# Decoder step on one core: the third and fourth delta-rule unit 14 and 10 slots later, convolution blocks alternating between them, two steps of every unit a slot further apart

## Chip, core and metric

One core of one Trainium2 chip. The metric is the device time of one launch in microseconds (us), the median of three runs. The core has a matrix engine (PE, with its weight loads as PEld), two vector engines (DVE, and POOL, which is GpSimd), a scalar engine for activation functions (ACT), and SP, which here only issues DMAs. Each engine runs its own instructions in order and waits on semaphores for the others.

## What is computed

One layer of a decoder step for 256 prompt tokens and 8 sample tokens, model width 2048. Four token mixers run in parallel on one input projection, their outputs are gated, summed and projected, then come cross-attention and a squared-ReLU MLP.

```python
proj = x @ p["w_in"] + p["b_in"]
...
o_a, S_a_new = gated_delta_rule(q_a, k_a, v_a, beta, g, S_a)        # A, 8 heads, chunks of 64
u_b, conv_b_new = causal_dwconv(a_b * jax.nn.sigmoid(g_b), conv_b, p["b_conv_w"])   # B, width 31
u_c, conv_c_new = causal_dwconv(cg_c * h_c, conv_c, p["c_conv_w"])  # C, width 3
h, C_new, n_new, m_new = mlstm_chunked(q, k, v, i_d.astype(f32), ...)               # D
y = jnp.sum(gates * proj_br, axis=2) @ p["w_out"]
```

In branch A each chunk needs `qk`, a lower triangular system `a_low`, its inverse, and then a recurrence over the four chunks of the prompt.

## The kernel before

All big products are cut into 704 **slots**. A slot is one 512 KB piece of weights (`raw`, 128 x 1024 floats) that SP loads, ACT rounds to `wh`, and DVE (for every fourth slot POOL) reduces to the rest `wl = raw - wh`; PE then does 24 matmuls with it (`xh*wh`, `xl*wh`, `xh*wl` for 8 blocks of 128). Splitting runs two slots ahead of the matmuls. `gin` is an input projection of 128 columns: two slots and a `post` that takes the result from PSUM.

Beside the slots stand Python generators. Once per slot the loop in `run` takes one step of the first generator of `chain`, and as many steps of `fill` as a planned DVE time (`dv_t` against `pe_t`, costs in `cost`) allows; a planned DVE time that is too far ahead skips the step of `chain` in that slot. `drain` takes all remaining steps of a generator at once. What the steps emit is then put in each engine's order by the tile scheduler, so a step's instructions can stand some slots behind the slot in which they were emitted.

- `a_gemm(u)` projects the six blocks (q, k, v of two heads) of unit `u` and `a_block` post-processes each: a width-4 convolution (`cu` on DVE), a sigmoid, a product on POOL. After the sixth, `a_unit(u)` is put on `chain`. There are four units, 0 to 3 (the third and fourth of the title are units 2 and 3); only one is in progress at a time. `a_begin(u)` drains unit `u - 2`, since two buffers `qkv` are shared by the four.
- `a_unit` first normalises q and k (`unit_rms`: a square and a split on ACT and POOL, the sums `ssl2q`, `ssl2k` on PE, logarithm and exponential on ACT, a DVE product), then computes `KQ` and decays, builds `m_u`, `m_a`, `m_t` on DVE, inverts in five levels (`xb`, then `ub` and `tb`), and runs the four chunks (`ks`, `db`, `ob`, `sb`), in between the state update of the samples (`s_upd`, which reads `dbc` from a DMA), and last a norm (`ssrm`). `unit_rms` keeps its result in a tile `rr` of which there is one.
- `b_block(j)` (two `gin`, four slots) puts `b_conv(j)` on `fill`: 30 DVE instructions `cB` of 128 x 256. `c_block(j)` has three `gin`, six slots, and little DVE work.
- `phase2(2, "C", True)` follows, from slot 128 on: gates by a sigmoid on ACT (`gate`) and a `merged` product on DVE, with no convolutions.

Slots before: unit 0 has slots 0 to 11, unit 1 12 to 23, blocks 0 and 1 of B and C 24 to 43, unit 2 44 to 55, blocks 2 to 4 56 to 85, unit 3 86 to 97, blocks 5 to 7 98 to 127.

Of the kernel before, what the change touches and what calls it, by code (L numbers as in the profile page):

```python
# [91 lines left out]
def decoder_step(ctx, tc, A, O):  # L92
# [15 lines left out]
    def bank(name):  # L108
        return pb.tile([P, 512], F32, tag="b", name=name)
# [6 lines left out]
    def cost(ap, rate=1.0):  # L116
        n = 1
        for x in ap.shape[1:]:
            n *= x
        dv_t[0] += 0.07 + n * rate / 960.0  # L120

    def act(out, in_, func, bias=0.0, scale=1.0, **kw):
        return AC.activation(out, in_, func, bias=bias, scale=scale, **kw)  # L123

    def tt(out, a, b, op, eng=None):
        if eng is None:
            cost(out)
        return (eng or DV).tensor_tensor(out=out, in0=a, in1=b, op=op)  # L128

    def ts(out, a, s1, op0, s2=None, op1=None):  # L130
        cost(out, 0.6)
        if op1 is None:
            DV.tensor_scalar(out, a, s1, None, op0=op0)
        else:
            DV.tensor_scalar(out, a, s1, s2, op0=op0, op1=op1)

    def stt(out, a, s, b, op0, op1):
        cost(out, 1.1)
        return DV.scalar_tensor_tensor(out=out, in0=a, scalar=s, in1=b, op0=op0, op1=op1)  # L139
# [9 lines left out]
    def mm(out, lhsT, rhs, start=True, stop=True):  # L149
        PE.matmul(out, lhsT, rhs, start=start, stop=stop)  # L150
# [3 lines left out]
    def split(hi, lo, src):  # L154
        act(hi, src, AF.Copy)
        tt(lo, src, hi.bitcast(F32), SUB)
# [9 lines left out]
    def sigmoid(g, src, bias=None):  # L166
        if bias is None:
            ts(g, src, -80.0, MAX)
        else:
            ts(g, src, bias, ADD, -80.0, MAX)  # L170
        act(g, g, AF.Exp, scale=-1.0)
        act(g, g, AF.Ln, bias=ones[:, 0:1])
        act(g, g, AF.Exp, scale=-1.0)
# [17 lines left out]
    def col(name, i=0, n=1):  # L191
        o, w = _pc[name]
        return pc[:, o + i:o + i + n]

    def con(name):
        o, w = _cc[name]
        return cst[:, o:o + w]
# [25 lines left out]
    def drain(g):  # L223
        for q in (chain, fill):
            while g in q:
                step(q)
# [12 lines left out]
    def later(n, f):  # L239
        todo.append((now[0] + n, f))  # L240

    def store(dst, src):
        later(DELAY, lambda: dma(dst, src))
# [127 lines left out]
    def gin(start, post):  # L371
        i = BI[start]
        gemm(A["win"][i - 1], xs, 2, lambda ps: post(ps, col("bin", i)))
# [63 lines left out]
    c1 = w1.tile([P, 2, 4, 8], F32, name="c1")  # L437
    c2 = w1.tile([P, 2, 4, 8], F32, name="c2")
    c3 = w1.tile([P, NCH, 2], F32, name="c3")
# [155 lines left out]
    def sconv(win, wc, W, dst, eng=None):  # L595
        t = tp.tile([P, NS, W], F32, tag="cw%d" % W, name="cw", bufs=1)
        tt(t[:], win, wc[:, None, :].to_broadcast([P, NS, W]), MUL, eng=GP)
        DV.reduce_sum(out=dst, in_=t[:], axis=AX.X)
        cost(t[:])
# [8 lines left out]
    def selc(h):  # L608
        return selw[:, h, :]
# [45 lines left out]
    def colb(ct, g, h, n, shape):  # L655
        return ct[:, :, g, h:h + n, None].to_broadcast(shape)

    def mat(name):
        return w1.tile([P, 2, 2, CH], F32, tag=name, name=name)

    def each():
        for hf in range(2):
            for hh in range(2):
                for c in range(2):
                    yield hf, hh, slice(CH * c, CH * c + CH), slice(hf * P + c * CH, hf * P + c * CH + CH)

    def v4(b):
        return b[:, :256].rearrange("p (f h l) -> p f h l", f=2, h=2)
# [19 lines left out]
    def a_unit(u):  # L688
# [7 lines left out]
        yield from unit_rms(k, 1.0, "l2k", res)  # L696
        tt(k, k, res[1][:], MUL)
        yield
        G = bank("G")[:].rearrange("p (h s f l) -> p h s f l", h=2, s=2, f=2)
        KQ = bank("KQ")[:].rearrange("p (f h s l) -> p f h s l", f=2, h=2, s=2)  # L700
        for hh in range(2):
            mm(G[:, hh], selc(h0 + hh), RA[:])
        Gs = [G[:, :, s].rearrange("p h f l -> p f h l") for s in range(2)]
        for hf, hh, o, t in each():
# [17 lines left out]
        for dst, src, m in ((U, U, "m1u"), (T, Am, "m1t")):  # L722
            tt(dst[:], src[:], con(m)[:, None, None, :].to_broadcast(sh), MUL)
            tt(dst[:], dst[:], con("eye")[:, None, None, :].to_broadcast(sh), ADD)
        yield
        sv = [P, 2, 2, P]
        v5 = lambda b: b[:].rearrange("p (f h l) -> p f h l", f=2, h=2)
# [164 lines left out]
    def newpair(name):  # L892
        return xp.tile([P, 2, NB, NT], F32R, tag="x16", name=name)
# [3 lines left out]
    def c_block(j):  # L897
        st = {}

        def post_h(ps, bc):  # L900
            if j == 0:
                drain(rowg[0])
                pr["C"] = newpair("pairC")
            st["h"] = tp.tile([P, NT], F32, tag="ht", name="ht", bufs=1)
            act(st["h"][:], ps, AF.Identity, bias=bc)

        def post_c(ps, bc):
            e = tp.tile([P, 30 + NT], F32, tag="ext", name="extC", bufs=1)
            GP.memset(e[:, 0:2], 0.0)
            stt(e[:, 2:2 + NT], ps, bc, st["h"][:], ADD, MUL)  # L910
            GP.tensor_copy(winC[:, j, :, 2], e[:, 2 + NP:2 + NT])
            GP.tensor_copy(scp[:, j, :], e[:, NP:NP + 2])
            wc = col("cC", 3 * j, 3)
            v = tp.tile([P, NT], F32, tag="cu", name="cuC", bufs=1)
            act(v[:, 0:NP], e[:, 0:NP], AF.Copy, scale=wc[:, 0:1])
            for i in range(1, 3):
                stt(v[:, 0:NP], e[:, i:i + NP], wc[:, i:i + 1], v[:, 0:NP], MUL, ADD)
            sconv(winC[:, j], wc, 3, v[:, NP:])
            st["v"] = v

        def post_b(ps, bc):
            v = st["v"]
            stt(v[:], ps, bc, v[:], ADD, MUL)
            split(pr["C"][:, 0, j, :], pr["C"][:, 1, j, :], v[:])
            if j == NB - 1:
                store(O["sc_p"], scp[:])
                store(O["sc_s"], winC[:])

        gin(O_H + P * j, post_h)
        gin(O_CG + P * j, post_c)  # L930
        gin(O_BG + P * j, post_b)
# [19 lines left out]
    def win_b(j):  # L951
        bst["w"] = tp.tile([P, NS, 31], F32, tag="winB", name="winB", bufs=2)
        dma(bst["w"][:], A["sB"][:, j])

    def b_block(j):
        st = {}

        def post_a(ps, bc):
            if j == 0:
                bst["cB"] = w1.tile([P, NB, NT], F32, tag="h8", name="cB", bufs=2)  # L960
                bst["ln"] = Norm(bst["cB"], NB, "B", w1, True)
            st["a"] = tp.tile([P, NT], F32, tag="ht", name="at", bufs=1)
            act(st["a"][:], ps, AF.Identity, bias=bc)

        def post_g(ps, bc):
            if j >= 2:
                drain(bgen[j - 2])
            g = tp.tile([P, NT], F32, tag="sg", name="gB")
            sigmoid(g[:], ps, bc)
            e = tp.tile([P, 30 + NT], F32, tag="extB", name="extB")  # L970
            win = bst["w"]
            if j < NB - 1:
                later(3, lambda: win_b(j + 1))
            GP.memset(e[:, 0:30], 0.0)
            tt(e[:, 30:], st["a"][:], g[:], MUL, eng=GP)
            GP.tensor_copy(win[:, :, 30], e[:, 30 + NP:])
            store(O["gl_p"][:, j], e[:, NP:NP + 30])
            store(O["gl_s"][:, j], win[:])
            dst = bst["cB"][:, j, NP:]
            sconv(win, col("cB", 31 * j, 31), 31, dst)  # L980
            ts(dst, dst, col("bcb", j), ADD)
            bgen[j] = b_conv(j, e)
            fill.append(bgen[j])

        gin(O_GLU + P * j, post_a)
        gin(O_GLU + BW + P * j, post_g)
# [84 lines left out]
    def d_unit(u):  # L1071
# [4 lines left out]
        KQ = v4(bank("KQd"))  # L1076
        G = bank("Gd")[:, :256].rearrange("p (h f l) -> p h f l", h=2, f=2)
        for hh in range(2):
            mm(G[:, hh], selc(h0 + hh), RD[:])
        for hf, hh, o, t in each():  # L1080
            mm(KQ[o, hf, hh], k[:, hh, t], q[:, hh, t])
        E, QK = mat("m_dl"), mat("m_dt")
        tt(E[:], G.rearrange("p h f l -> p f h l"), colb(c1, 3, h0, 2, sh), SUB)
        ts(E[:], E[:], 0.0, MAX)
# [180 lines left out]
        for i in range(4 if u == 0 else 0, 6):  # L1265
            gin(O_QKV + P * ((i // 2) * 8 + 2 * u + i % 2), a_block(u, i))

    def bc(js):
        for j in js:
            b_block(j)  # L1270
            c_block(j)

    a_gemm(0)
    a_gemm(1)
    bc((0, 1))
    a_gemm(2)
    bc((2, 3, 4))
    a_gemm(3)
    bc((5, 6, 7))
    phase2(2, "C", True)  # L1280
    bng = b_norm()
    mark(lambda: chain.append(bng))
# [570 lines left out]
```

## Time and profile before

| | us |
|---|---|
| median of three runs (2324.32 to 2328.25) | 2326.68 |
| the profiled execution, device time | 2324.7 |
| its span in the trace | 2322.9 |

What is read below comes from the profiled execution. The mean granted clock of PE is 0.990 of full speed in it. Slot numbers are counted from the weight matmuls in the trace, 24 to a slot: the blocks of unit 2 begin at 170 us, those of unit 3 at 336 us, phase 2 at 495 us, slot 176 at 665 us.

### The profile page before, as it was taken

The page shows a single profiled execution, that of the slowest core. Times are in us where ns is not written, and L with a number is a line of the kernel's source. Part 1 is how long each engine was busy: PE and PEld are TensorE (multiplying, and loading weights), DVE is VectorE, ACT ScalarE, POOL GpSimd, SP SyncE. Part 2 cuts the span into 40 slices and gives each one's busy share as a digit, 9 for nine tenths or more (in the row PEclk, how much of TensorE's full clock was granted, in tenths as well). Part 3 has the DMA queues.
Part 4 walks back from the last instruction along what each step waited for, and adds up shares of the span by engine and source line. Part 5 has one row for each costly group of instructions (what it writes and reads, how often), then busy time and mean ns, then how long its engine had stood idle before and what let it go on. Part 6 is the DMA issues. An engine that isn't in the chain of part 4 may idle for free.

```text
span 2322.9 us, 46442 instructions
## 1 busy us (share of the span) xinstructions
PE 2249.0 (97%) x19034; PEld 2205.4 (95%) x19034; DVE 1269.8 (55%) x2039; ACT 1167.0 (50%) x1789; POOL 977.8 (42%) x733
## 2 busy tenths in 40 slices
PE   9899999989999999999989999989999999999997
PEld 8899898989999999999989998889999999999997
DVE  7998998894464455433474566385323323323323
ACT  6756456554554455544434555456435435534543
POOL 4535335341222133433243365165445544544576
PEclk9999999999999999999999999999999999999998
DMA  7556455554656676765556666545565565566553
GB/s 233 166 151 201 137 174 167 169 165 143 193 173 185 195 221 215 211 182 182 182 183 182 200 200 201 187 132 181 181 182 176 179 182 181 174 183 181 176 180 127
DMA packets 125134, 418.81 MB, mean 180 GB/s; under 512 B 15608, under 2 KB 20984, under 8 KB 124920
## 3 DMA queue, kind: packets, MB, share of 16 engines
q1 hardware_dynamic: 124920, 415.84, 58.4%
q8 instruction: 149, 2.44, 0.4%
q14 instruction: 65, 0.53, 0.1%
HBM read 401.37 MB, written 14.41 MB: 179 GB/s over the span
## 4 chain that ended last, share of the span: by engine, by line
PE 81%; DVE 13%; issue 3%; DMA 1%; ACT 1%; POOL 1%; DVEq 0%; POOLq 0%; ACTq 0%; SPq 0%
PE g L150 73%; DVE cB L139 3%; DVE wl L128 3%; PE q L150 1%; DVE cu L139 1%; DVE y L128 1%; PE pv L150 1%; DVE y L139 1%; DMA dbc<-dd 1%; PE ub L150 0%; PE xb L150 0%; DVE s L139 0%; PE cb L150 0%; ACT wh L123 0%; PE nb L150 0%
## 5 line engine op out<-in xcount | busy, mean ns | idle before, releaser
L123 ACT ACTIVATE wh<-raw 128x1024 fp32r<-128x1024 f32 (+1 forms) x705 | 745.4, 1058 | 822.4 <-PE g L150 306.3
L128 POOL TENSOR_TENSOR wl<-raw,wh 128x1024 fp32r<-128x1024 f32 x240 | 588.0, 2450 | 724.7 <-PE g L150 483.2
L150 PE MATMUL g<-xh,wl 128*128 128x264 f32 x2496 | 714.0, 286 | 8.1 <-DVE wl L128 6.0
L150 PE MATMUL g<-xl,wh 128*128 128x264 f32 x2496 | 717.2, 287 | 0.0
L150 PE MATMUL g<-xh,wh 128*128 128x264 f32 x2496 | 716.1, 287 | 0.9 <-ACT wh L123 0.9
L128 DVE TENSOR_TENSOR wl<-raw,wh 128x1024 fp32r<-128x1024 f32 (+1 forms) x465 | 589.8, 1269 | 231.2 <-PE g L150 169.6
L150 PEld LDWEIGHTS g<-xh,wl 128*128 128x128 f32 x2496 | 473.0, 190 | 10.2 <-DVE wl L128 6.6
L150 PEld LDWEIGHTS g<-xh,wh 128*128 128x128 f32 x2496 | 473.5, 190 | 5.3 <-issue 2.5
L150 PEld LDWEIGHTS g<-xl,wh 128*128 128x128 f32 x2496 | 472.2, 189 | 2.3 <-issue 1.3
L150 PE MATMUL g<-hgh,wl 128*128 128x264 f32 x1024 | 290.4, 284 | 0.0
L150 PE MATMUL g<-hgl,wh 128*128 128x264 f32 x1024 | 290.4, 284 | 0.0
L150 PE MATMUL g<-hgh,wh 128*128 128x264 f32 x1024 | 289.9, 284 | 0.0
L150 PE MATMUL g<-zh,wh 128*128 128x266 f32 x960 | 275.1, 287 | 0.8 <-DVE zw L128 0.8
L150 PE MATMUL g<-zl,wh 128*128 128x266 f32 x960 | 274.6, 286 | 0.0
L150 PE MATMUL g<-zh,wl 128*128 128x266 f32 x960 | 274.4, 286 | 0.0
L150 PEld LDWEIGHTS g<-hgl,wh 128*128 128x128 f32 x1024 | 193.0, 188 | 0.0
L150 PEld LDWEIGHTS g<-hgh,wh 128*128 128x128 f32 x1024 | 192.5, 188 | 0.0
L150 PEld LDWEIGHTS g<-hgh,wl 128*128 128x128 f32 x1024 | 192.4, 188 | 0.0
L128 DVE TENSOR_TENSOR y<-y,g 128x264 f32<-128x264 f32 x80 | 34.3, 429 | 278.7 <-PE g L150 278.7
L150 PEld LDWEIGHTS g<-zh,wh 128*128 128x128 f32 x960 | 181.4, 189 | 1.0 <-ACT wh L123 1.0
L150 PEld LDWEIGHTS g<-zl,wh 128*128 128x128 f32 x960 | 181.7, 189 | 0.0
L150 PEld LDWEIGHTS g<-zh,wl 128*128 128x128 f32 x960 | 180.8, 188 | 0.0
(481 smaller groups left out, 3449.3 us busy)
## 6 DMA issues: line engine op xcount, KB each, us to landing
raw<-in_win_dram SPq DMA_DIRECT2D x312, 512.0 KB, 4.0
raw<-in_f_dram SPq DMA_DIRECT2D x248, 512.0 KB, 4.2
raw<-in_wbr_dram SPq DMA_DIRECT2D x64, 512.0 KB, 4.0
raw<-in_wout_dram SPq DMA_DIRECT2D x32, 512.0 KB, 4.3
s<-in_sS_dram SPq DMA_DIRECT2D x8, 512.0 KB, 5.0
dbc<-dd SPq DMA_DIRECT2D x16, 256.0 KB, 3.7
out_S_s_dram<-s SPq DMA_DIRECT2D x8, 512.0 KB, 5.2
c<-in_sCm_dram SPq DMA_DIRECT2D x8, 512.0 KB, 5.7
```

Source lines behind the costliest of these rows:

```text
L123: return AC.activation(out, in_, func, bias=bias, scale=scale, **kw)
L128: return (eng or DV).tensor_tensor(out=out, in0=a, in1=b, op=op)
L139: return DV.scalar_tensor_tensor(out=out, in0=a, scalar=s, in1=b, op0=op0, op1=op1)
L150: PE.matmul(out, lhsT, rhs, start=start, stop=stop)
```

## The change

Two steps get one slot more distance: an empty `yield` between the product that ends k's norm and `KQ`, and one between the building of `m_u`, `m_t` and the first level. A unit so has 38 steps where it had 36. And the order of the projections is another: blocks of B and C are still alternated, but seven of them now stand before unit 2, five between unit 2 and unit 3, four behind.

```diff
         tt(k, k, res[1][:], MUL)
         yield
+        yield
         G = bank("G")[:].rearrange("p (h s f l) -> p h s f l", h=2, s=2, f=2)
...
             tt(dst[:], dst[:], con("eye")[:, None, None, :].to_broadcast(sh), ADD)
+        yield
         yield
...
-    def bc(js):
-        for j in js:
-            b_block(j)
-            c_block(j)
+    def bc(order):
+        for f in order.split():
+            (b_block if f[0] == "b" else c_block)(int(f[1]))
 
     a_gemm(0)
     a_gemm(1)
-    bc((0, 1))
+    bc("b0 c0 b1 c1 b2 c2 b3")
     a_gemm(2)
-    bc((2, 3, 4))
+    bc("c3 b4 c4 b5 c5")
     a_gemm(3)
-    bc((5, 6, 7))
+    bc("b6 c6 b7 c7")
```

Slots after: blocks b0 to b3 and c0 to c2 24 to 57, unit 2 58 to 69, c3 to c5 with b4 and b5 70 to 95, unit 3 96 to 107, the last four blocks 108 to 127. From slot 176 on the five engines' orders are the same as before. Emitted steps of the units (first to last slot) before: 19 to 45, 47 to 83, 84 to 120, 121 to 158; now: 19 to 58, 59 to 97, 98 to 137, 138 to 175. Of unit 0's 36 steps before, ten are taken at once in slot 45, by the drain in `a_begin(2)`; now two steps of unit 1 are, in slot 97.

DVE's order at the end of unit 0, before: two of its state updates (`s`, four instructions each) with a step of the recurrence (`S`) between them, in short succession.

```order
L139 SCALAR_TENSOR_TENSOR s_1422<-dbc,qkv,s_1422 128x128 x4
L139 SCALAR_TENSOR_TENSOR cB<-extB,pc,cB 128x256
L139 SCALAR_TENSOR_TENSOR S<-S,gl,sb 128x128 x2
L128 TENSOR_TENSOR wl<-raw,wh 128x1024
L139 SCALAR_TENSOR_TENSOR cB<-extB,pc,cB 128x256
L139 SCALAR_TENSOR_TENSOR s_1424<-dbc,qkv,s_1424 128x128 x4
L139 SCALAR_TENSOR_TENSOR cu<-extA,pc,cu 128x256
```

The same place of DVE's order now:

```order
L139 SCALAR_TENSOR_TENSOR s_1496<-dbc,qkv,s_1496 128x128
L139 SCALAR_TENSOR_TENSOR cB<-extB,pc,cB 128x256 x2
L128 TENSOR_TENSOR wl<-raw,wh 128x1024
L139 SCALAR_TENSOR_TENSOR cB<-extB,pc,cB 128x256 x3
L139 SCALAR_TENSOR_TENSOR S<-S,gl,sb 128x128 x2
L139 SCALAR_TENSOR_TENSOR cB<-extB,pc,cB 128x256
L139 SCALAR_TENSOR_TENSOR extC<-g,pc,ht 128x264
L128 TENSOR_TENSOR wl<-raw,wh 128x1024
```

The updates are spread over more slots, and the instructions of B's third convolution (`cB`) stand between them.

DVE's order in the projections of unit 2, before: the six blocks' small convolutions (`cu`) stand between splits (`wl`) alone.

```order
L128 TENSOR_TENSOR wl<-raw,wh 128x1024 x2
L139 SCALAR_TENSOR_TENSOR S<-S,gl,sb 128x128 x2
L598 TENSOR_REDUCE cu<-cw 128x8
L139 SCALAR_TENSOR_TENSOR cu<-extA,pc,cu 128x256
L598 TENSOR_REDUCE cu<-cw 128x8
L139 SCALAR_TENSOR_TENSOR cu<-extA,pc,cu 128x256 x4
L133 TENSOR_SCALAR sg<-cu 128x264
```

The same blocks in DVE's order now:

```order
L128 TENSOR_TENSOR wl<-raw,wh 128x1024
L139 SCALAR_TENSOR_TENSOR cu<-extA,pc,cu 128x256
L139 SCALAR_TENSOR_TENSOR cB<-extB,pc,cB 128x256
L133 TENSOR_SCALAR sg<-cu 128x264
L128 TENSOR_TENSOR qkv<-qkv,rl2k 128x528
L139 SCALAR_TENSOR_TENSOR cB<-extB,pc,cB 128x256
L128 TENSOR_TENSOR wl<-raw,wh 128x1024
L128 TENSOR_TENSOR qkp<-qkv 128x16
L139 SCALAR_TENSOR_TENSOR cB<-extB,pc,cB 128x256
L139 SCALAR_TENSOR_TENSOR cu<-extA,pc,cu 128x256
```

B's fourth convolution and the norms of unit 1 (`qkv`, `qkp`) now share DVE with them. In the 16 slots from the first block on DVE has 91 instructions before, 15 of them `cB`, and now 103, 35 of them `cB`.

ACT's order at the norm of k in unit 3, before: the only norm at the head of a unit that stands beside the gates of phase 2.

```order
L123 ACTIVATE sql2k<-rl2k 128x528
L123 ACTIVATE wh<-raw 128x1024 x2
L123 ACT_TABLE_LOAD
L123 ACTIVATE gate<-g,pc 128x264
L123 ACT_TABLE_LOAD
L123 ACTIVATE rl2k<-ssl2k,eps 128x2x256
L123 ACTIVATE rl2k<-ss2l2k,eps 128x2x8
L123 ACT_TABLE_LOAD
```

ACT's order at the norm of q in unit 3 now (the norms of k and the last norm of unit 2 look alike):

```order
L123 ACTIVATE sql2q<-rl2q 128x528
L123 ACTIVATE wh<-raw 128x1024 x2
L123 ACT_TABLE_LOAD
L123 ACTIVATE gate<-g,pc 128x264
L123 ACT_TABLE_LOAD
L123 ACTIVATE rl2q<-ssl2q,eps 128x2x256
L123 ACTIVATE rl2q<-ss2l2q,eps 128x2x8
L123 ACT_TABLE_LOAD
L123 ACTIVATE rl2q<-rl2q 128x528
```

More norms now stand between gates, and each brings loads of activation tables with it: 22 in the whole program, 16 before.

## Rows read from the trace of the kernel before

**Rows 1.** The page: busy time, share of the span and instructions by engine.
```profile
PE 2249.0 (97%) x19034; PEld 2205.4 (95%) x19034; DVE 1269.8 (55%) x2039; ACT 1167.0 (50%) x1789; POOL 977.8 (42%) x733
```
**Rows 2.** The chain that ended last: start, us, engine, tile, line, number.
```profile
609.52 58.28 PE g L150 x480
```
**Rows 3.** Windows: length, busy time and count by engine, PE clock, DMA share, GB/s.
```profile
44.80:93.10 48.30, 40.72 (x321) 39.35 (x321) 45.09 (x78) 37.15 (x71) 29.89 (x38) 0.96 0.48 143
93.00:171.00 78.00, 75.96 (x798) 72.87 (x798) 71.52 (x132) 44.34 (x84) 30.16 (x39) 1.00 0.54 162
229.00:336.00 107.00, 100.33 (x985) 96.91 (x985) 98.55 (x180) 52.37 (x93) 39.21 (x43) 0.98 0.54 161
378.00:495.00 117.00, 111.36 (x1089) 108.00 (x1089) 102.40 (x191) 62.37 (x111) 46.34 (x50) 1.00 0.53 161
495.00:523.00 28.00, 23.97 (x196) 22.84 (x195) 26.68 (x45) 17.21 (x22) 10.29 (x7) 0.94 0.58 181
523.00:600.00 77.00, 77.00 (x800) 74.92 (x800) 33.35 (x59) 33.50 (x59) 12.71 (x8) 1.00 0.49 145
284.50:291.50 7.00, 5.08 (x41) 4.92 (x40) 6.71 (x17) 3.70 (x11) 0.26 (x1) 0.76 0.23 77
```
**Rows 4.** PE's waits from 93 to 171 us: tile, releaser, us, times, longest.
```profile
PE xb L150 <- DVE m_u L128: 1.3, 1, 1.3
```
**Rows 5.** PE's waits from 171 to 229 us, projections of unit 2.
```profile
PE ks L150 <- DVE S L139: 2.9, 2, 2.0
```
**Rows 6.** PE's waits from 229 to 336 us, unit 1.
```profile
PE xb L150 <- DVE m_u L818: 2.8, 3, 1.9
PE db L150 <- DVE vt L139: 2.1, 2, 1.2
PE xb L150 <- DVE m_u L128: 1.8, 1, 1.8
```
**Rows 7.** PE's waits from 336 to 378 us, projections of unit 3, head of unit 2.
```profile
PE ssl2q L150 <- ACT sql2q L123: 1.7, 1, 1.7
```
**Rows 8.** PE's waits from 378 to 495 us, unit 2 and the start of unit 3.
```profile
PE ssl2q L150 <- ACT sql2q L123: 2.6, 1, 2.6
PE KQ L150 <- DVE qkv L128: 2.3, 1, 2.3
```
**Rows 9.** PE's waits from 495 to 665 us, unit 3.
```profile
PE KQ L150 <- DVE qkv L128: 3.0, 1, 3.0
PE xb L150 <- DVE m_u L128: 0.8, 1, 0.8
```
**Rows 10.** DVE in order of time near the first level of unit 3.
```profile
518.24 0.41 DVE L128 TENSOR_TENSOR m_dt<-KQ,m_dt 128x256 f32<-128x256 f32 x1
518.57 2.28 DVE L128 TENSOR_TENSOR m_u<-m_u,cst 128x256 f32<-128x256 f32 x1
```
**Rows 11.** POOL in order of time at the same place.
```profile
517.99 2.58 POOL L128 TENSOR_TENSOR wl<-raw,wh 128x1024 fp32r<-128x1024 f32 x1
```
**Rows 12.** ACT's groups from 93 to 665 us: busy us, mean ns, idle before.
```profile
L123 ACT ACTIVATE wh<-raw 128x1024 fp32r<-128x1024 f32 x153 | 161.4, 1056 | 162.6 <-PE g L150 91.0 <-DMA raw<-in_win_dram 52.6 <-DMA raw<-in_wbr_dram 10.4
L123 ACT ACT_TABLE_LOAD x7 | 9.0, 1283 | 0.1
```
**Rows 13.** ACT in order of time, start of unit 3 and its norm of k.
```profile
489.46 0.64 ACT L123 ACTIVATE rl2q<-qkv 128x528 f32<-128x528 f32 x1 [5.30 <-DVE oA L139]
...
506.77 1.28 ACT L123 ACT_TABLE_LOAD   x1
508.06 0.69 ACT L123 ACTIVATE rl2k<-ssl2k,eps 128x512 f32<-128x512 f32 x1
```
**Rows 14.** DVE's groups from 93 to 523 us.
```profile
L139 DVE SCALAR_TENSOR_TENSOR cB<-extB,pc,cB 128x256 f32<-128x256 f32 x240 | 146.6, 611 | 8.1 <-ACT cB L123 4.3
L128 DVE TENSOR_TENSOR wl<-raw,wh 128x1024 fp32r<-128x1024 f32 x83 | 108.3, 1306 | 5.9 <-PE g L150 3.6 <-issue 2.0 <-ACT wh L123 0.3
L139 DVE SCALAR_TENSOR_TENSOR cu<-extA,pc,cu 128x256 f32<-128x256 f32 x46 | 34.3, 753 | 3.3 <-ACT cu L123 2.9
```

## The prediction

> **What bounds the kernel now.** The page comes first: PE is busy for 97% of the span [rows 1]. That share says where to look, not how much is left, so I ask what a slot costs when nothing waits. The chain that ended last has an undisturbed piece in phase 2: 480 weight matmuls in 58.28 us [rows 2], 0.1214 us each, 2.914 us for a slot of 24. No matmul is added or removed here, so the time can only change by PE's waits. The change touches emitted steps from slot 24 to 175, roughly 93 to 665 us; from slot 176 on the order is the same.
>
> The windows by stretch tell what PE waits for there. Up to 523 us DVE is busy for 71.5 of 78, 98.6 of 107, 102.4 of 117 and 26.7 of 28 us, that is 92, 92, 88 and 95%; behind it, 33.4 of 77, 43% [rows 3]. As long as convolutions run DVE is almost full, and a chain step that passes through it stands in a queue. With the start of phase 2 this ends.
>
> PE's waits, stretch by stretch: 1.3 in unit 0 [rows 4], 2.9 at the drain [rows 5], 2.8 + 2.1 + 1.8 in unit 1 [rows 6], 1.7 at the head of unit 2 [rows 7], 2.6 + 2.3 later [rows 8], 3.0 + 0.8 in unit 3 [rows 9]: **21.3 us** (those under 0.8 are left out on both sides). Two of them bring a slower clock with them: 0.76 over 7 us around 288 us and 0.94 over 28 us at 495 us [rows 3], so 7 x 0.24 = 1.7 and 28 x 0.06 = 1.7 us. In all some **24.7 us** stand to be won, 1.1% of the time.
>
> **How I price a wait that stays.** A small matmul waits less if more weight matmuls stand before it, 0.1214 us for each. I counted those in both orders, from the matmul group that starts the chain step to the one that waits, and take the wait of before less the difference. Where another place of before is nearer by its count or its load on DVE, I take that one.
>
> **Unit 0.** From `KQ` to the first `xb` there were 57, now 66: 1.3 - 9 x 0.121 = 0.2. From the norm to `KQ` 55 without a wait, now 49: between 0 and 0.7, I take 0.3. The drain goes: its ten steps put two `ks` behind state updates [rows 5], which are now spread. So 2.9 goes, but the chunk steps now run beside B's third convolution. The nearest row is the 2.1 us of `db` beside such convolutions in unit 1 [rows 6]; bounds 0 and 2.1, I take 1.0. Together 1.5 where there were 4.2.
>
> **Head of unit 1, the new load.** Unit 2's six blocks stood alone with 15 `cB` in 16 slots; now there are 35, and 103 DVE instructions where there were 91. What that costs is the largest unknown. In the one stretch where such blocks had a full DVE, 78 instructions took 45.1 us, 0.58 each [rows 3]; 103 are 59.5 us. PE needs 16 x 2.914 = 46.6 and, by estimate from the small groups elsewhere, 5 more. DVE is 8 us short. Splits lead by two slots, 5.8 us, and part of that is already used up: the wait lies between 0 and 8, I take 5.0, nearer to the upper end since 88 to 95% on DVE leave little lead. The norm of q: 72 matmuls after the last norm, close to the 75 that waited 1.7 [rows 7], so 2.0. Then B's fourth convolution is over, and from slot 76 on the small groups of unit 1 stand at the starts of slots, where the scheduler has put them because they were emitted there, not because they were late. Of 2.8 + 2.1 + 1.8 [rows 6] I leave 0.5. Together 7.5 where there were 6.7.
>
> **Unit 2.** It again starts beside the blocks of the next unit. Norm of q 65 for 75: 1.7 + 10 x 0.121 = 2.9. `KQ` 58 for 52: 2.3 - 0.7 = 1.6. First `xb` 57 for 65 without a wait: 1.0. Together 5.5 where there were 4.0.
>
> **Unit 3.** It starts at slot 138, when all convolutions are over and DVE is at 43%. The 2.6 before it was ACT's first square, which waited 5.30 us for DVE's last product of unit 2, `oA` [rows 13], because the tile `rr` is shared; that product stood behind `cB`. Now 72 matmuls for 53 give 2.6 - 2.3 = 0.3. `KQ` has 46 for 51, which alone would make 3.0 into 3.6; but DVE no longer queues. Bounds 0 and 3.6, I take 1.0. The first `xb`: 72 for 55, 0. Together 1.3 where there were 6.4.
>
> Here the cover has to be named. Norms beside gates make ACT change tables: six loads more, 1.283 us each [rows 12], 7.7 us of ACT. They are hidden by ACT's idle time: 33.5 of 77 us are busy [rows 3]. But not with much room. In three slots (8.74 us) ACT has three `wh` at 1.056, a gate, three loads at 1.283 and the norm's own four or five instructions of about 0.65, near 10 us, for four norms in a row; the lead of two to three slots of `wh` takes up this lag of some 1.3 us a norm. If that cover is gone, 7.7 us are lost. The Trainium skill, page "ScalarE: Activation LUTs", section "What ACT_TABLE_LOAD costs", speaks against the change more strongly: with the drain a switch costs 2.66 us, so six are 16 us by this estimate, and the change would lose what it wins. The trace differs: a load begins at 506.77, lasts 1.28 us, and the next activation starts at 508.06 [rows 13], with no drain between; the row decides.
>
> **The sum.** Waits: 1.5 + 7.5 + 5.5 + 1.3 = 15.8. One fall of the clock in place of two, 1.7. So 17.5 in place of 24.7: **7.2 us less**. The profiled execution, 2324.7, would become 2317.5; the median of the runs stands 2.0 above it, so 2326.7 - 7.2 = **2319.5 us**.
>
> **Rivals.**
>
> *More is won.* The splits' lead covers the new load in unit 1 wholly, with no fall of the clock: 5.0 + 1.7 more, and unit 2 waits only as before, 1.5 more. 15.4 in all: 2311. For it: the stretch from 229 us had a DVE as full and waited 6.7 us for three chain steps only. Against it: the `cu` work comes in bursts.
>
> *The waits come back* (no change). What makes a chain step late is often not its distance but POOL. DVE's `m_u`, 0.41 us for a like instruction, took 2.28 us at 518.57, from a time when POOL's split of 2.58 us had begun [rows 10, 11], and the first level of unit 3 waited. A slot more moves a step to another place against every fourth slot's split, and may put it under one as well as out. If what I let the distances win comes back (1.1 of `xb` in unit 0, 2.3 of the levels in unit 1, 2.3 + 2.0 + 0.8 in unit 3), 8.5 us are lost again: 2328. The Trainium skill, page "SBUF — State Buffer", section "Who interferes with whom", has it as a rule: DVE and GpSimd share a port pair under an exclusive lock, and the loser is blocked for the other's whole instruction. By that rule, and the trace agrees with 2.28 us against 0.41, distance is no cure. Against this rival: in phase 2 most DVE work is gone, so one blocked instruction does not delay a queue.
>
> *Slower.* Blocks beside convolutions overload DVE for good. At the means of their groups [rows 14] the 35 `cB`, 12 `wl` and 18 `cu` take 21.4 + 15.7 + 13.6 = 50.7 us, the other 38 at 0.41 some 15.6, together 66.3 against PE's 51.6: 14.7 short, 9.7 more than I took. Unit 3's blocks have 94 instructions for 84, 0.58 x 10 = 5.8 us more. If neither is absorbed, 15.5 - 7.2 = 8.3 us are lost: 2335. It is decided at slots 58 to 74: if PE waits there for about 15 us, this holds; for under 8, it doesn't. Against it: durations overlap, so sums of means are too long, and DVE's load between slots 76 and 90 is low.
>
> **How the numbers follow.** A difference of 0.2%, 4.7 us, is about what a measurement of this kernel can tell from none. The forecast has 0.44, more is won 0.18, waits come back 0.24, slower 0.14. Faster than 2322: most of the first (0.40) and all of the second, 0.58. Within 0.2%: the rest of the first and the waits that come back, 0.28. Slower: 0.14. The forecast's own range follows from the bounds of its four open terms: 5.0 + 0.3 + 1.0 + 1.0 = 7.3 less or 3.0 + 0.4 + 1.1 + 2.6 = 7.1 more, 2312 to 2327. The whole range reaches past it to the two outer cases and leaves out about 2 in 10: 2308 to 2330.
>
> **What would show each step.** Right: no `ks` wait at the end of unit 0; unit 3's `ssl2q` and `KQ` together under 2 us; 13 table loads from 93 to 665 us with no wait for `wh`; unit 1's levels without waits. Wrong: PE waits at slots 58 to 74 of over 8 us, or waits of `KQ` and first `xb` as long as before with a long DVE instruction just ahead of them.

## The result and the profile after

| | median, us | lowest to highest | ratio to before, 95% interval |
|---|---|---|---|
| before, 4 runs beside it | 2327.34 | 2324.32 to 2328.25 | |
| changed kernel, 4 runs | 2339.32 | 2336.25 to 2340.48 | 1.0052 [1.0034, 1.0069] |

The change makes the kernel slower by 0.52%, 12.1 us of 2327. The profiled execution has 2340.48 us and a span of 2338.7.

Where the time goes is read from the slots: the time at which the first weight matmul of a slot starts. In the profiled executions of both kernels:

| slots | what stands there | before, us | after, us | difference |
|---|---|---|---|---|
| 24 to 60 | unit 0 | 135.6 | 137.2 | +1.6 |
| 60 to 98 | unit 1 | 148.9 | 150.6 | +1.7 |
| 98 to 176 | units 2 and 3, with phase 2 from slot 128 | 287.2 | 295.4 | +8.2 |
| 176 to 240 | the end of the change's reach | 207.3 | 208.8 | +1.5 |

So +13.0 us in all, most of it where I had unit 3 cheap. Part of a difference can be work that has moved: slots 98 to 128 have 337 small matmuls (all but the 24 of a slot) where before has 371, slots 128 to 176 have 417 for 373. PE is busy there for 171.52 us, before for 165.67, so some 0.13 us for each, by an estimate. Over slots 98 to 176 together it is 754 for 744, which is why they stand in one row. And a difference of under 3 us in one stretch is not clear: the kernel before and an edit of it below, which alters only the gates of phase 2, have the same orders up to slot 128 and differ by 2.9 us in slots 24 to 98. The page first, the busy times by engine, which answer to [rows 1]:

```profile
PE 2256.6 (96%) x19034; PEld 2212.5 (95%) x19034; DVE 1267.1 (54%) x2039; ACT 1174.7 (50%) x1795; POOL 981.1 (42%) x733
```

The instructions of PE and DVE are the same in number; ACT has six more, the table loads. Now the windows by stretch (columns as in [rows 3]). The first five are slots 24 to 44, 44 to 60, 60 to 98, 98 to 128 and 128 to 176. Then come two pairs of 7 us each, one after the other, 226 to 240 and 541 to 555 us.

```profile
93.80:172.80 79.00, 75.17 (x777) 71.89 (x776) 72.58 (x135) 42.47 (x80) 29.62 (x38) 0.98 0.51 156
172.80:231.00 58.20, 56.31 (x465) 55.76 (x463) 52.34 (x90) 28.46 (x46) 21.56 (x21) 1.00 0.56 170
231.00:381.50 150.50, 140.76 (x1289) 136.89 (x1287) 123.81 (x220) 77.34 (x137) 67.87 (x78) 0.97 0.54 163
381.50:498.20 116.70, 108.85 (x1060) 104.86 (x1059) 99.19 (x173) 65.70 (x121) 52.13 (x64) 1.00 0.53 161
498.20:676.90 178.70, 171.52 (x1571) 167.59 (x1570) 94.39 (x157) 95.07 (x137) 38.48 (x23) 0.99 0.55 169
226.00:233.00 7.00, 4.80 (x37) 4.33 (x35) 6.89 (x10) 4.62 (x8) 4.92 (x5) 1.00 0.30 73
233.00:240.00 7.00, 5.09 (x28) 4.99 (x29) 4.04 (x10) 4.40 (x8) 4.66 (x8) 0.76 0.89 307
541.00:548.00 7.00, 4.84 (x40) 4.62 (x39) 0.63 (x2) 6.91 (x9) 0.00 (x0) 1.00 0.36 122
548.00:555.00 7.00, 5.46 (x32) 5.32 (x33) 3.48 (x4) 4.20 (x6) 3.63 (x2) 0.76 0.37 92
```

DVE is nearly full up to slot 60 and in slots 98 to 128 (85 to 92%), less so in between (82%, where before has 91%), and half idle behind slot 128 (94.39 of 178.70). ACT is not full anywhere over a whole stretch (95.07 of 178.70), but in the seven microseconds from 541 on it is busy for 6.91, and DVE for 0.63: there PE and DVE wait for ACT. PE idles for 2.2 us in each of the two upper pieces, and in the piece that follows its mean clock is 0.76. Five such pieces lie between 93 and 690 us (the others at 162, 266 and 363); the profiled execution of before has two.

PE's waits from 93 to 690 us (columns as in [rows 4]):

```profile
PE g L150 <- DVE wl L128: 4.4, 3, 2.5
PE ssl2k L150 <- ACT sql2k L123: 4.3, 2, 3.7
PE db L150 <- DVE vt L139: 4.1, 3, 2.6
PE xb L150 <- DVE m_u L128: 3.8, 3, 2.0
PE ssl2q L150 <- POOL sql2q L128: 3.0, 1, 3.0
PE KQ L150 <- DVE qkv L128: 2.7, 2, 2.1
PE xb L150 <- DVE m_u L820: 2.0, 2, 1.5
PE ssl2q L150 <- ACT sql2q L123: 1.9, 2, 1.2
PE ub L150 <- ACT m_dl L123: 1.9, 2, 1.7
PE m L150 <- DVE cB L139: 1.4, 1, 1.4
PE ssl2k L150 <- POOL sql2k L128: 1.1, 1, 1.1
```

They come to 30.6 us. The same view of the kernel before comes to 23.9 ([rows 4 to 9] hold 21.3 of it, without the small ones). So the waits are 6.7 us longer and the slower clock costs some 5 us more (three pieces more, 7 x 0.24 us each): 11.7 of the 13.0. The `ks` of [rows 5] is gone. In its place stand waits for ACT's `sql2k` (3.7 in unit 3), for POOL's `sql2q` (3.0 in unit 1) and for splits (`wl`).

The longest one, ACT in order of time at the head of unit 3 (the number in brackets is the idle time before an instruction):

```profile
540.36 1.06 ACT L123 ACTIVATE wh<-raw 128x1024 fp32r<-128x1024 f32 x1 [1.10 <-DMA raw<-in_wbr_dram]
541.44 1.28 ACT L123 ACT_TABLE_LOAD   x1
542.73 0.48 ACT L123 ACTIVATE gate<-g,pc 128x264 f32<-128x264 f32 x1
543.23 1.28 ACT L123 ACT_TABLE_LOAD   x1
544.53 0.69 ACT L123 ACTIVATE rl2q<-ssl2q,eps 128x512 f32<-128x512 f32 x1
545.11 0.27 ACT L123 ACTIVATE rl2q<-ss2l2q,eps 128x16 f32<-128x16 f32 x1
545.40 1.28 ACT L123 ACT_TABLE_LOAD   x1
546.69 0.64 ACT L123 ACTIVATE rl2q<-rl2q 128x528 f32<-128x528 f32 x1
547.24 1.04 ACT L123 ACTIVATE wh<-raw 128x1024 fp32r<-128x1024 f32 x1
548.19 0.63 ACT L123 ACTIVATE rl2k<-qkv 128x528 f32<-128x528 f32 x1
548.85 0.64 ACT L123 ACTIVATE sql2k<-rl2k 128x528 fp32r<-128x528 f32 x1
```

This is a single file: three loads, the gate between the first two, then logarithm, load, exponential, and only then the square of k's norm, for whose `sql2k` PE stands still. None of the loads runs beside other ACT work, and nothing else of the norm can run meanwhile. PE's last matmul of `ssl2q` ends at 538.2, the norm's exponential at 547.3, 9.1 us later. The same three loads stand again from 554.27 on, and `KQ` waits 2.1 us.

The wait for POOL, in POOL's order of time at slot 60:

```profile
228.04 1.22 POOL L128 TENSOR_TENSOR cB<-cB,m 128x264 f32<-128x264 f32 x1 [4.93 <-DVE cB L139]
229.20 0.10 POOL L632 MEMSET extA<- 128x3 f32 x1
229.34 1.60 POOL L128 TENSOR_TENSOR a0B<-a0B,cB 128x264 f32<-128x264 f32 x1
230.90 1.72 POOL L128 TENSOR_TENSOR a0B<-a0B,ln_z 128x264 f32<-128x264 f32 x1
232.59 2.27 POOL L128 TENSOR_TENSOR sql2q<-rl2q,sql2q 128x528 fp32r<-128x528 f32 x1
```

Unit 1's `sql2q`, for which PE waits, stands behind the three products that end a convolution of B. And a level of unit 0, in DVE's order of time at slot 41.7, where `xb` waits 1.5:

```profile
154.88 1.21 DVE L128 TENSOR_TENSOR wl<-raw,wh 128x1024 fp32r<-128x1024 f32 x1
156.01 5.59 DVE L139 SCALAR_TENSOR_TENSOR cB<-extB,pc,cB 128x256 f32<-128x256 f32 x7
161.53 0.43 DVE L820 COPY_PREDICATED m_u<-mint,ub 128x256 f32<-128x256 uint8 x1
```

The level's `m_u` stands behind seven `cB` in a row.

**Theories.** Four are open. *Table loads*: the norms of unit 3 now stand among the gates, and the loads of ACT's tables cost time because they lie in the chain from one norm to the next. *Alignment*: the two yields do not lengthen distances so much as move every later step to another place among POOL's instructions and DVE's bursts of `cB`, at a loss here. *Units too late*: two steps more in each unit push it into phase 2, so that order and yields are one cause. *ACT time*: the six loads take time that `wh` needs.

### The profile page after: what moved, and what is told of

It is laid out like the page before. It is cut to its first block, busy times and chain, and to the rows that moved or that the text cites. A ratio compares the mean times of both kernels' runs of the same rounds, so it can differ in the third digit from the quotient of the medians.

```text
span 2338.7 us, 46460 instructions
## 1 busy us (share of the span) xinstructions
PE 2256.6 (96%) x19034; PEld 2212.5 (95%) x19034; DVE 1267.1 (54%) x2039; ACT 1174.7 (50%) x1795; POOL 981.1 (42%) x733
## 4 chain that ended last, share of the span: by engine, by line
PE 75%; DVE 15%; issue 4%; ACT 2%; POOL 2%; DMA 2%; DVEq 0%; SPq 0%; ACTq 0%; POOLq 0%
PE g L150 68%; DVE cB L139 3%; DVE wl L128 3%; DVE cu L139 2%; PE q L150 1%; DVE y L128 1%; PE pv L150 1%; DMA raw<-in_win_dram 1%; ACT wh L123 1%; DVE y L139 1%; DVE s L139 1%; DMA dbc<-dd 1%; PE ub L150 0%; PE cb L150 0%; DVE cuC L139 0%
## 5 line engine op out<-in xcount | busy, mean ns | idle before, releaser
L150 PEld LDWEIGHTS g<-xh,wl 128*128 128x128 f32 x2496 | 475.1, 190 | 15.7 <-DVE wl L128 12.1
L150 PE MATMUL g<-hgh,wl 128*128 128x264 f32 x1024 | 290.4, 284 | 0.0
L150 PE MATMUL g<-hgl,wh 128*128 128x264 f32 x1024 | 290.4, 284 | 0.0
```

## The experiments

Each was timed beside the kernel before on the same chip, in 5 or 11 runs; a stretch in microseconds is from the one profiled execution. A gain or a loss in microseconds is the ratio times 2327. A single ratio is uncertain by 0.0009 to 0.0018, some 2 to 4 us.

### Order and yields apart

The new order alone:

```diff
         tt(k, k, res[1][:], MUL)
         yield
-        yield
...
             tt(dst[:], dst[:], con("eye")[:, None, None, :].to_broadcast(sh), ADD)
-        yield
         yield
```

> The new order of the projections alone, without the two empty yields. Theory 'order': the order has taken the drain away and so puts unit 3's head (q norm, k norm, KQ) into the gates of phase 2; without the yields the units still end at slot 170 (before: 158, changed kernel: 175), so nearly all of the 12 us stays: 2335 to 2341. Theory 'yields': two steps more in each unit, eight in all, have pushed the units late; then this kernel is within 3 us of before, 2324 to 2330.

Measured: 2332.02, ratio 1.0021 [1.0012, 1.0030], +4.9 us.

The two yields alone are the same lines, added to the kernel before.

> The old order with the two empty yields in each unit. Theory 'order': this costs little, 2324 to 2330, and may win a little, since KQ and the first level wait for less (before: 1.3 for xb in unit 0, 2.3 for KQ in unit 2, 3.0 for KQ in unit 3). Theory 'yields': 2335 to 2341.

Measured: 2330.78, ratio 1.0020 [1.0011, 1.0028], +4.7 us; its profiled execution, with 2336.66, is the slowest of its eleven.

Both theories were wrong by half: each part costs about 5 us by itself. The stretches say where the order's lie: in slots 24 to 98 it takes 280.5 us, before 284.5, so it wins 4.0; in slots 98 to 176 it takes 296.2 for 287.2 and loses 9.0. The changed kernel has 287.8 and 295.4: beside the new order the yields take 7.3 in the first stretch and nothing in the second (and the 1.5 behind slot 176, which the order alone hasn't). Other executions of kernels with the same orders up to slot 128 have 280.5 and 280.6 in slots 24 to 98 with the order alone, 285.0 and 287.5 with the yields added, and 287.4 with neither, so the win there is 4.0 to 6.9 and the yields' loss 4.5 to 7.3. The yields alone lose in both stretches of their one execution (290.9 and 292.9), with no table load more than before (16). So the order loses behind slot 98, the yields beside the convolutions at least, and they are two causes.

### Gates without table changes

In the changed kernel, and for a control in the kernel before, the gates of the first phase 2 by exponential, logarithm, exponential:

```diff
-                last["SIG"] = act(st["s"][:], ps, AF.Sigmoid, bias=bc)
+                if first:
+                    sigmoid(st["s"][:], ps, bc)
+                else:
+                    last["SIG"] = act(st["s"][:], ps, AF.Sigmoid, bias=bc)
```

> The changed kernel, with the 16 gates of the first phase 2 by exp, ln and exp in place of a sigmoid, so that the ACT tables are not changed there: 7 loads in the program's order for 22. It pays for that with two activations of 128x264 and one DVE instruction more in each gate. Theory 'table loads': the 9.0 us that slots 128 to 176 lost, 3.9 for ssl2k and 2.2 for KQ in unit 3 and a clock window, come from loads of 1.28 us that stand in the chain from one norm to the next; then it gains 5 to 9 us: 2330 to 2334. Rival 'place': the waits of unit 3 have other causes (POOL, DVE, distance); then it is within 3 us of the changed kernel or slower by the added work, 2337 to 2345.

> Control of the former: the kernel before with the same gates without table changes, 7 loads for 16. Theory 'table loads': before had one norm at the head of a unit beside the gates, with 3.0 us at KQ of unit 3, so it gains 1 to 4 us here: 2323 to 2326, less than the changed kernel gains. Rival 'place': no gain, or a loss by the added ACT and DVE work, 2326 to 2335.

Measured: 2330.94, 1.0015 [1.0006, 1.0024] for the changed kernel, so 8.6 us less than without the edit; 2324.22, 0.9988 [0.9979, 0.9997] for the kernel before, 2.8 less. This is what *table loads* expected of both. In slots 128 to 176 the changed kernel takes 173.1 in place of 178.7, with the same small matmuls, and the wait for `sql2k` is gone.

With the same edit on the order alone:

> The new order without the two yields, with gates that need no table change (7 loads). It puts together what the order wins before slot 98 (2.2 us by slot 60, 1.8 more by 98) and takes out what it loses in slots 128 to 176. Theory 'table loads': 2332.0 less 6 to 8, so 2324 to 2326, no slower than before. Rival 'place': the loss in phase 2 is of another kind, and it stays at 2330 to 2335.

Measured: 2323.00, 0.9984 [0.9975, 0.9993]: faster than before by 3.7 us, the lowest ratio of all, and 8.6 less than the order alone. So without table changes the order costs nothing (2323.00 beside 2324.22 of the control); the yields still cost 7.2 us: 1.0015 beside 0.9984.

### More loads, but off the chain

The edit above also changes what a gate is. This one leaves the gates and adds loads:

```diff
                 last["SIG"] = act(st["s"][:], ps, AF.Sigmoid, bias=bc)
+                if first:
+                    last["SIG"] = after(AC.preload_act_table_set("natural_log_exp_and_others"), "SIG")
```

> The changed kernel, with the table for logarithm and exponential loaded again right behind each gate of the first phase 2: 39 loads in the program's order for 22, so some 22 us more of ACT (17 x 1.283), but the Exp of a norm no longer stands behind a load of its own. Theory 'place' (a load costs only where it stands between two steps of a norm): 1.28 us less in the way of each of unit 3's norms, so it gains 2 to 6 us on the changed kernel, 2333 to 2337. Theory 'time' (the loads take ACT time that wh needs): slower than the changed kernel by 3 to 15 us, 2342 to 2355.

Measured: 2328.19, 1.0003 [0.9994, 1.0012]. With 17 loads more the changed kernel is 11.4 us faster, and no different from before. *ACT time* is refuted. The gain is also more than the 2 to 6 us that *place* expected for one load less in each norm. The windows of slots 128 to 176 and PE's waits there, of this kernel:

```profile
497.30:667.70 170.40, 169.61 (x1571) 166.19 (x1570) 93.62 (x157) 120.11 (x156) 39.04 (x23) 1.00 0.58 177
```

```profile
PE db L150 <- DVE vt L139: 0.5, 1, 0.5
PE ssl2k L150 <- ACT sql2k L123: 0.3, 1, 0.3
```

ACT is busy for 120.11 of 170.40 us where it was busy for 95.07 of 178.70, 70% for 53%, and PE waits for 0.8 us where it waited for 7.2. ACT in order of time at the head of unit 3, beside the rows of the changed kernel above:

```profile
537.35 1.28 ACT L123 ACT_TABLE_LOAD   x1
538.64 0.48 ACT L123 ACTIVATE gate<-g,pc 128x264 f32<-128x264 f32 x1
539.14 1.28 ACT L1015 ACT_TABLE_LOAD   x1
540.43 0.69 ACT L123 ACTIVATE rl2q<-ssl2q,eps 128x512 f32<-128x512 f32 x1
541.02 0.27 ACT L123 ACTIVATE rl2q<-ss2l2q,eps 128x16 f32<-128x16 f32 x1
541.18 1.06 ACT L123 ACTIVATE wh<-raw 128x1024 fp32r<-128x1024 f32 x1
542.13 0.64 ACT L123 ACTIVATE rl2q<-rl2q 128x528 f32<-128x528 f32 x1
```

No load stands between logarithm and exponential, and the first of the two that are left starts while PE is still at `ssl2q`, whose last matmul ends at 538.3. The exponential ends at 542.8, 4.5 us later, in place of 9.1. Only 1.28 of these 4.6 us are the load that is gone. The rest lies in the order around it and in what ACT waits for there: between `sql2q` and the first load stands one `wh` where there were two (the other has moved ahead of `sql2q`), and another now runs between logarithm and exponential. The edit so moves `wh` as well as loads, and no run here parts the two.

The Trainium skill, page "ScalarE: Activation LUTs", section "Table sets: the hidden batching unit", says that logarithm then exponential need one load, since one set holds both. The changed kernel's trace differs, with a load ahead of each (543.23 and 545.40); here, with that set loaded by name, the trace agrees.

The same edit on the order alone:

> The new order without the yields, with the table for logarithm and exponential loaded again behind each gate of the first phase 2 (39 loads). By 'place' it gains on the order alone (2332.0) what that did for the changed kernel or a little less, 7 to 11 us: 2321 to 2325, as good as gates without table changes. By 'time' it is slower than the order alone, 2333 to 2345.

Measured: 2325.00, 0.9991 [0.9982, 1.0000], 7.0 less than the order alone. The yields then cost 2.8 us (1.0003 beside 0.9991), less than the 7.2 beside the other gates; with intervals of some 3 us on each, the runs hardly tell the two apart.

### One yield at a time

The new order with the first of the two yields (ahead of `KQ`), and with the second (ahead of the first level); each is the diff of the order alone with one of its two lines left out.

> The new order with the yield ahead of KQ alone. The changed kernel is 7 us above the order alone (2332.0). Theory 'level yield': what the yields lose is the second one's, which puts a level of unit 0 behind seven cB in a row (1.6 us at slot 41.7) and the mean of cB behind DVE; so this kernel is near the order alone, 2330 to 2334. Rival 'either': each yield only moves all later steps against the splits on POOL and the bursts of cB, so each costs some; 2334 to 2338.

> The new order with the yield ahead of the first level alone. Theory 'level yield': most of the 7 us is here, 2335 to 2340. Rival 'either': 2333 to 2337, about as much as the yield ahead of KQ costs.

Measured: 2332.70, 1.0025 [1.0016, 1.0034], and 2333.60, 1.0027 [1.0018, 1.0035]. Beside 1.0021 without yields and 1.0052 with both, neither alone costs anything that is clear (0.9 and 1.4), and both together cost 7.2. The medians don't add up, but the intervals are too wide to show that they can't. In slots 24 to 98 the two kernels take 283.1 and 282.2, between 280.5 and 287.7. The traces show one reason: PE's wait for unit 1's norm of q is 1.1 or 1.2 us in slot 59 with either yield, and 4.1 in slot 60 with both, where `sql2q` comes behind the convolution's end on POOL.

### That wait taken away

The changed kernel with unit 1's `sql2q` on DVE:

```diff
-    def unit_rms(x, scale, name, res):
+    def unit_rms(x, scale, name, res, e=GP):
...
-        tt(lo[:], r[:], hi[:].bitcast(F32), SUB, eng=GP)
+        tt(lo[:], r[:], hi[:].bitcast(F32), SUB, eng=e)
...
-        yield from unit_rms(q, 1.0, "l2q", res)
+        yield from unit_rms(q, 1.0, "l2q", res, None if u == 1 else GP)
```

> The changed kernel, with one instruction on another engine: the split sql2q of unit 1's norm of q on DVE in place of POOL. In the changed kernel it stands on POOL behind three products of a convolution's end (1.22, 1.60 and 1.72 us) and takes 2.27 us itself while DVE splits weights, and PE waits 1.3 and 3.1 us for it at slot 60. Theory 'place on POOL': that wait goes, 2 to 4 us less than the changed kernel, 2335 to 2337. Rival 'DVE is full there': DVE does it no earlier, or its splits then come late, and the time stays within 1.5 us, 2338 to 2341.

Measured: 2338.13, 1.0045 [1.0032, 1.0057], 1.6 less than the changed kernel and not clearly apart from it. That is in the range of *DVE is full there*, but not for its reason. The wait is gone: slots 24 to 98 take 283.0 us in place of 287.8. But slots 98 to 176 take 299.3 in place of 295.4. PE's waits in 381 to 500 us of this kernel, the first three:

```profile
PE ssl2k L150 <- ACT sql2k L123: 2.4, 1, 2.4
PE ob L150 <- ACT dl L123: 2.2, 1, 2.2
PE ub L150 <- ACT m_dl L123: 2.1, 1, 2.1
```

What is won in one unit is given back in the next, by which path is not shown: `ob` stands in none of the changed kernel's waits above.

### POOL's splits two slots later

In the changed kernel, and for a control in the kernel before:

```diff
-        on_pool = len(slots) > 8 and seen[0] % every[0] == 0
+        on_pool = len(slots) > 8 and seen[0] % every[0] == (2 if 24 <= len(slots) < 176 else 0)
```

> The changed kernel with POOL's split in another one of each four slots (two later) in slots 24 to 175. Theory 'alignment': the waits of the units' steps hang on which slot's split they meet, so the single waits move by 1 to 4 us each and the sum changes by 2 to 6 us in either sign; the loss in slots 128 to 176 by table loads stays, at least 5 us over the 169.7 of before. Rival 'distance': the weight matmuls between the steps are the same, so the waits stay where they are, 2337 to 2341.

> Control of the former: the kernel before with POOL's split moved in the same way. Theory 'alignment': a change of 2 to 6 us in either sign with no change of the order. Rival 'distance': 2325 to 2328.

Measured: 2336.31, 1.0039 [1.0027, 1.0052] for the changed kernel, not clearly apart from it; slots 128 to 176 take 177.9, so the loss by table loads stays, as *alignment* said. (The 169.7 of before is no fair measure for it, since 44 small matmuls more stand there now; the changed kernel without that loss takes 170.4 to 173.1.) The kernel before becomes 2331.95, 1.0019 [1.0010, 1.0028], +4.4 us: with no step, no distance and no block moved, and with three table loads less (13), it loses as much as by the new order. Its waits in slots 24 to 98 come from other places:

```profile
PE db L150 <- DVE vt L139: 5.3, 2, 3.6
PE xb L150 <- DVE m_u L128: 4.0, 3, 1.8
PE xb L150 <- DVE m_u L818: 2.7, 3, 1.4
PE ks L150 <- DVE S L139: 1.9, 1, 1.9
```

`db`, the longest with 3.6, waited 1.2 before [rows 6].

## Why the prediction was wrong

Forecast 2319.5 in a range of 2308 to 2330; measured 2339.32. I gave 0.14 to slower. Two steps failed.

**The step that failed first** is the cover of the table loads: "They are hidden by ACT's idle time". The loads were counted rightly (six more at 1.283), and the price without that cover, "7.7 us are lost", lies near what gates without table changes (8.6) and loads put off the chain (11.4) give back. That is luck in part: it took all ACT time of the loads as lost, and 17 loads more lost nothing. A share of busy time is no cover for a load between two dependent steps. Raising ACT's share from 53 to 70% made the kernel faster. I forecast 1.3 us of waits for unit 3; it has 7.2 in slots 128 to 176, and `ssl2q` and `KQ`, which I had as the waits to look at, are less of it than `ssl2k`. With the loads out of the way the changed kernel still stands at 2328 to 2331 and wins nothing; that is the second step.

The Trainium skill, page "ScalarE: Activation LUTs", section "What ACT_TABLE_LOAD costs", adds a drain to each load. The trace differs here as well: the load at 541.44 lasts 1.28, and the next activation starts at 542.73.

**The step that failed second** is the price by distance ("0.1214 us for each" matmul). Single terms held: the first `xb` of unit 0 waits 0.2, as forecast, and `KQ` of unit 2 0.6 for 1.6. But what a yield won at its own place came back elsewhere: 1.4 of `m` and 2.0 of the later `xb` in unit 0, 3.0 of `sql2q` in unit 1, 1.7 each of `ssl2k` and `ub` in unit 2. The sum of the waits was to be 15.8 and is 25.4, if waits under 0.8 are left out as there (30.6 with them). Every term is too low: unit 0 has 2.9 for 1.5, unit 1 10.7 for 7.5, unit 2 5.9 for 5.5, unit 3 5.8 for 1.3. The rival that named this, *the waits come back*, had POOL as its cause and "may put it under one as well as out" as its argument. It was the nearest to what the yields did; its price of 8.5 lay near their 7.2, but it stood for a change of nothing, since I set it against 7.2 us that were to be won.

**Right** were the drain (no `ks` wait at the end of unit 0; the order alone is 2.2 us ahead by slot 60) and, in part, the levels of unit 1: one `xb` waits 1.5 us where I left 0.5 and before had 4.6, though `db` still waits 2.7. The order wins in slots 24 to 98, as I said. The thirteen loads up to slot 176 are there too.

**The new load at slots 58 to 74** I had at 5.0 with `ssl2q` at 2.0 beside it. There PE waits 4.1 for `ssl2q`, 2.5 for a split and 1.5 for `xb`, 8.1 in all. That is at the border I had set for *slower*. DVE's load was seen rightly: in slots 58 to 74 (223.5 to 290.4 us) it is busy for 59.2 us, where I had 59.5. But it costs PE 2.5 us by a split, not 5.0, and the longest wait, 3.0, is for POOL.

**The clock** was to fall once in place of twice, 1.7 us for 3.4; in the profiled execution it fell five times, 8.4 us by the same measure. The falls come with the waits, but how many there are differs between executions: the changed kernel with the added loads, whose orders agree with it up to slot 128, has three up to there where it has four.

So the 12.1 us are: the order with its loads 4.9 (a gain of some 4 in front, a loss of 9 in slots 98 to 176, of which 5 to 6 go when the loads leave the chain, and some 1.3, by the estimate above, are ten small matmuls that stood in front before), and the yields 7.2; alone the yields cost 4.7, and four pairs of kernels give them 2.8 to 7.2. That the loads among the norms are the cause of the first is shown by two different edits on two kernels; how much of it is the loads themselves and how much the `wh` that are placed around them is not. That the yields lose by alignment is shown for the wait at slot 60 and, by POOL's splits moved alone, for the size that such a shift can have; it is not shown wait by wait.

## What to carry to other kernels

A load or another short instruction that a switch of function brings is priced by what stands behind it in its engine's order, not by the engine's idle share; loading the table right behind the one function that evicts it costs more instructions and can still be faster. In a schedule as full as this one, a step more of distance is no gain that can be summed over places: ask which instruction of a shared engine each later step will now stand behind, and count with a loss as well as a gain. Before trusting a forecast of 0.3%, ask what a shift that should do nothing would do; here it was 0.19%.

## What was not expected of the hardware

Logarithm and exponential in a row brought two loads of 1.28 us where a sigmoid gate stood ahead of them, and none between them once the set that holds both was loaded by name. And a wait can be followed by a slower clock: after seven microseconds in which PE was busy for 4.80 or 4.84, the mean granted clock of the next seven was 0.76, some 3.4 us at the lower of the two levels (1.2 GHz), and 1.00 in the seven behind. But not every wait is: after a piece with 4.92 the clock stayed at 1.00.

```profile
555.00:562.00 7.00, 4.92 (x50) 4.55 (x48) 1.80 (x3) 6.93 (x9) 0.93 (x2) 1.00 0.35 132
562.00:569.00 7.00, 7.00 (x59) 7.00 (x58) 6.78 (x11) 3.61 (x7) 4.09 (x3) 1.00 0.54 153
```

What parts the two, these runs don't show.
